# Cached keys and memory rows rearranged from DRAM to DRAM ahead of the attention of a decoder step, with new step numbers for the attention's loads

## The chip, the core and the metric

The kernel runs on one NeuronCore of a Trainium2 chip. The engines named below are TensorE (PE, matmuls; PEld is its weight load), VectorE (DVE), ScalarE (ACT), GpSimd (POOL) and SyncE (SP, which here only issues DMAs). Each engine works through its own instructions in their built order. The metric is the device time of one execution in microseconds (us), a median over executions of one kernel.

## What is computed

One layer of a decoder for 256 prompt tokens and 8 samples of 4 tokens, which share all weights (D_MODEL 2048, float32):

```python
z = rms_norm(x, g_mix) @ w_in                      # 2048 x 11264: branch inputs and gates
y_a, y_b, y_c = chunk_mixer(..), conv_module(..), pool_mixer(..)
x = x + sum(sigmoid(gate) * (y @ w_branch)) @ w_out
q = rms_norm(x, g_xattn) @ w_xq                    # 4 heads of 512
# prompt:  k, v = rms_norm(mem) @ w_xk, rms_norm(mem) @ w_xv     (256 memory rows)
# sample b: k, v = cache_mem_k[b], cache_mem_v[b]                (256 x 4 heads x 512 each)
x = x + (softmax(q k^T / sqrt(512)) v) @ w_xo
x = x + relu(rms_norm(x, g_mlp) @ w_up)^2 @ w_down
y = rms_norm(x, g_final)
```

The keys and values of the prompt are outputs too. The cached keys and values are 16 MB each, the memory `mem_prompt` is 2 MB, and all weights together are some 340 MB, each read once.

## The kernel before

**Weights.** A plan made ahead lists every weight in pieces of 512 rows x 512 columns (1 MB, a `raw` tile). `load_w` (line 154) has SP load a piece. `split_w` cuts a piece into two halves of 256 rows, and for each half ACT writes a rounded copy `w_hi` (line 172) and DVE the rest `w_lo` (line 173). TensorE then makes three matmuls for each 128 x 128 block of weights (hi x hi, hi x lo, lo x hi: lines 239 to 241 for the stages with all 288 tokens, lines 274 to 276 in `proj_mem` for the keys and values of the prompt, with the 256 memory rows as stationary side and 512 weight columns streaming). There are three `raw` buffers and three each of `w_hi` and `w_lo`. The split of a half needs the buffer of the half three before it, so it starts when TensorE has finished that one; the load of a piece needs a `raw` buffer whose two halves are both split.

**Steps.** A clock counts steps: one half of a weight is one step. `later(n, fn)` puts a piece of other work n steps ahead, `at(step, fn)` at a step counted from `base`, the step at which the projection with `w_xk` starts. The projections with `w_out` and `w_xq` are steps -64 to 0, `w_xk` is 0 to 32, `w_xv` 32 to 64, `w_xo` follows. All this only sets the order in which the instructions stand on each engine; what an engine does when is decided by its waits.

**Keys of the samples.** 32 blocks of 512 KB, one for each sample and head. `k_load(n)` fills one of six `kv` tiles (128 x 1024) by four DMAs (line 852), each of which reads pieces of 128 floats (512 B) from the cache into 32 partitions. `k_transposed(n)` (line 859) transposes the tile in 32 x 32 blocks on DVE into a `kT` tile (nine buffers), and `k_scores(b)` (line 874) runs 32 small matmuls for the four heads of sample b. Loads 0 to 14 are spread over steps -62 to -6; load n from 15 on stands right behind the transposition of block n - 6, whose tile it takes, and blocks 9 to 31 are transposed between steps 1.5 and 20. Values: `v_load` (line 995) fills the same six tiles, 4 KB a partition, and `sample_values(b)` (line 1003) runs 16 matmuls for each sample, at steps 24, 29, ..., 59.

**Memory rows.** In the last quarter of `w_xq`, `mem_load` (line 905) brings a quarter of the memory (256 rows x 512) into a `raw` buffer. `mem_transposed` has ACT square it with a sum along the row (line 913), TensorE transpose it in eight 128 x 128 blocks into PSUM (line 918), and ACT and DVE make `m1`, its rounded copy times a gain and the rest (lines 197 and 200).

Of the kernel before, what the change touches and what calls it, by code (L numbers as in the profile page):

```python
# [38 lines left out]
def decoder_step_kernel(  # L39
# [23 lines left out]
    k_scr = dram.tile([MEM, DM], F32, name="k_scr")  # L63

# [814 lines left out]
    def score_step(b):  # L879
        return 1 + 2.5 * b  # L880

    def value_step(b):
        return 24 + 5 * b

    def k_step(n):
        if n < 9:
            return 4 * n - 60
        return score_step((n - 9) // 4) + 0.5 + 0.3 * ((n - 9) % 4)

    for n in range(32):  # L890
        at(4 * n - 62 if n < 15 else k_step(n - 6) + 0.2, lambda n=n: k_load(n))
        at(k_step(n), lambda n=n: k_transposed(n))
# [8 lines left out]
    mss = small.tile([P, 2, 4], F32, name="mss")  # L901

    def mem_load(qr):
        mraw = wpool.tile([P, 4, 512], F32, name="mraw", tag="raw")
        nc.sync.dma_start(mraw[:, :2], mem_prompt[0, :, qr * 512:(qr + 1) * 512].rearrange("(c p) n -> p c n", p=P))
        mbox[qr] = mraw

    def mem_transposed(qr):
        m1.add()
        mraw = mbox[qr]  # L910
        for c in range(2):
            junk = small.tile([P, 512], F32, name="junk", tag="kn", bufs=3)
            s_.activation(junk, mraw[:, c, :], AF.Square, accum_out=mss[:, c, qr:qr + 1])
        for k2 in range(0, 4, 2):
            pt = psum()
            for d in range(2):
                for c in range(2):
                    t_.transpose(pt[:, d * 256 + c * P:d * 256 + (c + 1) * P],
                                 mraw[:, c, (k2 + d) * P:(k2 + d + 1) * P], ident)
# [4 lines left out]
    def mem_rstd():
        ms = small.tile([P, 3], F32, name="ms")
        v_.reduce_sum(ms[:, :2], mss, axis=AX.X)
        v_.tensor_scalar(ms[:, :2], ms[:, :2], 1.0 / DM, RMS_EPS, ALU.mult, ALU.add)
        rpow(r_mem, ms[:, :2])
# [144 lines left out]
    at(20, sample_softmax)  # L1073
    at(21, sample_probs)
# [171 lines left out]
```

## Time and profile before

| What | Value |
|---|---|
| median of 3 executions | 2170.93 us (2165.51 to 2171.38) |
| the profiled execution | 2167.95 us, its span 2166.1 us |
| PE busy, PEld busy | 2132.5 us (98%), 2060.2 us (95%) |
| DVE, ACT busy | 1284.6 us (59%), 865.1 us (40%) |
| bytes moved by DMA | 397.50 MB, mean 184 GB/s |
| largest groups of DMA issues | 87 of `w_in`, 64 of `w_up`, 64 of `w_down`, 1024 KB each; 128 of cached keys, 128 KB each; 32 of cached values, 512 KB each |

The span runs from the first to the last instruction. The page cuts it into 40 slices and gives the busy share of each engine in tenths; PE and PEld rows show whether TensorE has work at every moment, and the rows on the clock and on DMA show what it got. Waits are listed with the instruction that waited and what released it.

### The profile page before, as it was taken

The page shows a single profiled execution, that of the slowest core. Times are in us where ns is not written, and L with a number is a line of the kernel's source. Part 1 is how long each engine was busy: PE and PEld are TensorE (multiplying, and loading weights), DVE is VectorE, ACT ScalarE, POOL GpSimd, SP SyncE. Part 2 cuts the span into 40 slices and gives each one's busy share as a digit, 9 for nine tenths or more (in the row PEclk, how much of TensorE's full clock was granted, in tenths as well). Part 3 has the DMA queues.
Part 4 walks back from the last instruction along what each step waited for, and adds up shares of the span by engine and source line. Part 5 has one row for each costly group of instructions (what it writes and reads, how often), then busy time and mean ns, then how long its engine had stood idle before and what let it go on. Part 6 is the DMA issues. An engine that isn't in the chain of part 4 may idle for free.

```text
span 2166.1 us, 36855 instructions
## 1 busy us (share of the span) xinstructions
PE 2132.5 (98%) x15559; PEld 2060.2 (95%) x15559; DVE 1284.6 (59%) x1955; ACT 865.1 (40%) x1189; POOL 31.3 (1%) x93
## 2 busy tenths in 40 slices
PE   8999999999999999998899999999999999999998
PEld 7999999999999999995677899999999999999997
DVE  7767877677565657555555646554454445545554
ACT  5444433343345434352334534333333333333343
POOL 1000000000000000001000000000000000000000
PEclk9999999999999999999899999999999999999999
DMA  7546444544545577769998554545554555455542
GB/s 248 192 150 212 159 156 156 168 164 158 174 157 174 201 216 206 203 195 233 284 335 278 178 167 157 174 158 174 157 174 157 174 158 173 159 172 160 172 156 103
DMA packets 223417, 397.50 MB, mean 184 GB/s; under 512 B 9402, under 2 KB 47930, under 8 KB 222843
## 3 DMA queue, kind: packets, MB, share of 16 engines
q1 hardware_dynamic: 218117, 384.37, 55.8%
q10 hardware_dynamic: 4878, 10.72, 1.4%
q8 instruction: 122, 2.00, 0.4%
q14 instruction: 44, 0.36, 0.1%
q0 software_dynamic: 256, 0.05, 0.0%
HBM read 383.51 MB, written 12.80 MB: 183 GB/s over the span
## 4 chain that ended last, share of the span: by engine, by line
PE 56%; issue 38%; DMA 4%; DVE 1%; SPq 1%; ACT 0%; POOL 0%; ACTq 0%; POOLq 0%; DVEq 0%
PE ps L241 15%; PE ps L239 15%; PE ps L240 15%; PE ps L274 2%; PE ps L275 2%; PE ps L276 2%; DMA kv<-in_cache_mem_k_dram 1%; DMA raw<-in_w_xk_dram 1%; PE ps L1003 1%; SPq L852 0%; DMA raw<-in_w_in_dram 0%; DVE w_lo L173 0%; PE ps L647 0%; ACT w_hi L172 0%; DMA k_scr<-kn 0%
## 5 line engine op out<-in xcount | busy, mean ns | idle before, releaser
L173 DVE TENSOR_TENSOR w_lo<-raw,w_hi 128x1024 fp32r<-128x1024 f32 (+1 forms) x673 | 785.5, 1172 | 818.3 <-ACT w_hi L172 815.4
L172 ACT CAST w_hi<-raw 128x1024 fp32r<-128x1024 f32 (+1 forms) x673 | 673.4, 1007 | 1156.6 <-PE ps L240 964.0
L239 PE MATMUL ps<-q_hi,w_hi 128*128 128x288 f32 x3200 | 946.9, 296 | 1.7 <-ACT w_hi L172 1.2
L241 PE MATMUL ps<-q_hi,w_lo 128*128 128x288 f32 x3200 | 943.7, 295 | 1.2 <-DVE w_lo L173 1.2
L240 PE MATMUL ps<-q_lo,w_hi 128*128 128x288 f32 x3200 | 943.4, 295 | 0.7 <-DVE q_lo L200 0.7
L239 PEld LDWEIGHTS ps<-q_hi,w_hi 128*128 128x128 f32 x3200 | 601.0, 188 | 3.1 <-ACT w_hi L172 1.4
L240 PEld LDWEIGHTS ps<-q_lo,w_hi 128*128 128x128 f32 x3200 | 601.2, 188 | 1.5 <-DVE q_lo L200 0.9
L241 PEld LDWEIGHTS ps<-q_hi,w_lo 128*128 128x128 f32 x3200 | 600.6, 188 | 1.7 <-DVE w_lo L173 1.6
L241 PE MATMUL ps<-h_hi,w_lo 128*128 128x288 f32 x1024 | 302.2, 295 | 0.0
L239 PE MATMUL ps<-h_hi,w_hi 128*128 128x288 f32 x1024 | 301.9, 295 | 0.0
L240 PE MATMUL ps<-h_lo,w_hi 128*128 128x288 f32 x1024 | 301.5, 294 | 0.0
L239 PEld LDWEIGHTS ps<-h_hi,w_hi 128*128 128x128 f32 x1024 | 192.1, 188 | 0.0
L240 PEld LDWEIGHTS ps<-h_lo,w_hi 128*128 128x128 f32 x1024 | 192.1, 188 | 0.0
L241 PEld LDWEIGHTS ps<-h_hi,w_lo 128*128 128x128 f32 x1024 | 192.1, 188 | 0.0
L274 PE MATMUL ps<-w_hi,q_hi 128*128 128x512 f32 x256 | 102.7, 406 | 11.4 <-ACT w_hi L172 11.4
L241 PE MATMUL ps<-y_hi,w_lo 128*128 128x288 f32 x384 | 113.3, 295 | 0.0
L240 PE MATMUL ps<-y_lo,w_hi 128*128 128x288 f32 x384 | 113.1, 294 | 0.0
L239 PE MATMUL ps<-y_hi,w_hi 128*128 128x288 f32 x384 | 113.0, 294 | 0.0
L527 DVE SCALAR_TENSOR_TENSOR cv<-glu,cwT,cv 128x256 f32<-128x256 f32 x240 | 105.9, 478 | 0.0
L275 PE MATMUL ps<-w_lo,q_hi 128*128 128x512 f32 x256 | 103.0, 402 | 1.7 <-DVE w_lo L173 1.7
L276 PE MATMUL ps<-w_hi,q_lo 128*128 128x512 f32 x256 | 101.5, 397 | 0.0
L274 PEld LDWEIGHTS ps<-w_hi,q_hi 128*128 128x128 f32 x256 | 48.6, 192 | 29.3 <-ACT w_hi L172 16.9
(301 smaller groups left out, 1277.1 us busy)
## 6 DMA issues: line engine op xcount, KB each, us to landing
raw<-in_w_in_dram SPq DMA_DIRECT2D x87, 1024.0 KB
raw<-in_w_up_dram SPq DMA_DIRECT2D x64, 1024.0 KB
raw<-in_w_down_dram SPq DMA_DIRECT2D x64, 1024.0 KB
raw<-in_w_branch_dram SPq DMA_DIRECT2D x24, 1024.0 KB
raw<-in_w_out_dram SPq DMA_DIRECT2D x16, 1024.0 KB
kv<-in_cache_mem_k_dram SPq DMA_DIRECT2D x128, 128.0 KB
raw<-in_w_xq_dram SPq DMA_DIRECT2D x16, 1024.0 KB
raw<-in_w_xk_dram SPq DMA_DIRECT2D x16, 1024.0 KB
```

Source lines behind the costliest of these rows:

```text
L172: latest["hi"] = s_.copy(dh, src)
L173: latest["lo"] = v_.tensor_tensor(dl, src, dh.bitcast(F32), ALU.subtract)
L239: t_.matmul(o, wh, act.hi(kt), start=kt == 0, stop=False)
L240: t_.matmul(o, wh, act.lo(kt), start=False, stop=False)
L241: t_.matmul(o, wl, act.hi(kt), start=False, stop=kt == nkt - 1)
L274: t_.matmul(acc[c], mh, hi[:, i, :], start=kt == 0, stop=False)
L275: t_.matmul(acc[c], mh, lo[:, i, :], start=False, stop=False)
L276: t_.matmul(acc[c], ml, hi[:, i, :], start=False, stop=kt == KT - 1)
L527: v_.scalar_tensor_tensor(o, i, wk, o, ALU.mult, ALU.add)
L1003: t_.matmul(sbox["osc"][32 * h:32 * h + 32, :], pTm[:, c, h, :], vraw[4 * b + 2 * c + h // 2][:, (h % 2) * 512:(h % 2 + 1) * 512], start=b ...
```

## The change

Three things are done.

1. **Copies.** `key_blocks` and `mem_blocks` are new. During the branches SP issues 128 DMAs of 128 KB (one each 1.4 steps from step 12 of the kernel on) that copy the cached keys from DRAM to DRAM, in pieces of 512 B, into 32 blocks `k_blk` in the layout of a `kv` tile; and 64 DMAs of 32 KB (one each 2.8 steps) that do so with the memory, in pieces of 128 B, into four blocks `m_blk`.
2. **Loads and the transposition of the memory.** `k_load` is then one DMA of 128 rows of 4 KB. `mem_load` reads a quarter of the memory in one DMA of 128 rows of 4 KB into one half of the `raw` tile, DVE transposes it in 32 x 32 blocks into the other half, and `m1` is made from there; the 32 transpositions by TensorE are gone. The sums of squares are made from four loads of 512 KB of `mem_prompt` at steps -63 to -61.5.
3. **Step numbers.** The scores of samples 4 to 7 move from steps 11 to 18.5 to steps 12, 18.5, 25 and 31.5; the values from 24 + 5b to 34.5 + 3.6b; key loads 15 to 31 stand at 1, 2.65, ..., 27.4, one each 1.65 steps; value loads 0.8 steps apart; the memory loads each one step earlier.

```diff
+    k_blk = [dram.tile([P, 1024], F32, name=f"k_blk{n}") for n in range(32)]
+    m_blk = [dram.tile([P, 1024], F32, name=f"m_blk{n}") for n in range(4)]
...
+    def mem_blocks(qr, k, qd):
+        c0 = qr * 512 + k * P + qd * 32
+        nc.sync.dma_start(m_blk[qr][32 * qd:32 * qd + 32, k * 256:(k + 1) * 256].rearrange("p (m r) -> p m r", r=32),
+                          mem_prompt[0, :, c0:c0 + 32].rearrange("(m p) r -> p m r", p=32))
+
+    def key_blocks(n, qd):
+        b, h = divmod(n, 4)
+        nc.sync.dma_start(k_blk[n][32 * qd:32 * qd + 32].rearrange("p (m r) -> p m r", r=P),
+                          cache_mem_k[0, b, :, h, qd * P:(qd + 1) * P].rearrange("(m p) r -> p m r", p=32))
+    for n in range(32):
+        for qd in range(4):
+            later(12 + (4 * n + qd) * 1.4, lambda n=n, qd=qd: key_blocks(n, qd))
+    for n in range(64):
+        later(12.5 + n * 2.8, lambda n=n: mem_blocks(n // 16, n // 4 % 4, n % 4))
...
+    mss = small.tile([P, 2, 2], F32, name="mss")
+
+    def mem_squares(c, half):
+        kv = kv_tile()
+        nc.sync.dma_start(kv, mem_prompt[0, c * P:(c + 1) * P, half * 1024:(half + 1) * 1024])
+        later(2, lambda: s_.activation(kv, kv, AF.Square, accum_out=mss[:, c, half:half + 1]))
...
     def k_load(n):
-        b, h = divmod(n, 4)
         kv = kv_tile()
-        for qd in range(4):
-            nc.sync.dma_start(
-                kv[32 * qd:32 * qd + 32].rearrange("p (m r) -> p m r", r=P),
-                cache_mem_k[0, b, :, h, qd * P:(qd + 1) * P].rearrange("(m p) r -> p m r", p=32))
+        nc.sync.dma_start(kv, k_blk[n])
         kraw[n] = kv
...
     def score_step(b):
-        return 1 + 2.5 * b
+        return 1 + 2.5 * b if b < 4 else 12 + 6.5 * (b - 4)
 
     def value_step(b):
-        return 24 + 5 * b
+        return 34.5 + 3.6 * b
+
+    def k_load_step(n):
+        return 3.9 * n - 59 if n < 15 else 1 + 1.65 * (n - 15)
 
     def k_step(n):
         if n < 9:
-            return 4 * n - 60
-        return score_step((n - 9) // 4) + 0.5 + 0.3 * ((n - 9) % 4)
+            return 3.9 * n - 56
+        return max(score_step((n - 9) // 4) + 0.5 + 0.3 * ((n - 9) % 4), k_load_step(n) + 2)
 
     for n in range(32):
-        at(4 * n - 62 if n < 15 else k_step(n - 6) + 0.2, lambda n=n: k_load(n))
+        at(k_load_step(n), lambda n=n: k_load(n))
         at(k_step(n), lambda n=n: k_transposed(n))
...
     def mem_load(qr):
         mraw = wpool.tile([P, 4, 512], F32, name="mraw", tag="raw")
-        nc.sync.dma_start(mraw[:, :2], mem_prompt[0, :, qr * 512:(qr + 1) * 512].rearrange("(c p) n -> p c n", p=P))
+        nc.sync.dma_start(mraw[:, :2], m_blk[qr].rearrange("p (t n) -> p t n", t=2))
         mbox[qr] = mraw
 
     def mem_transposed(qr):
         m1.add()
-        mraw = mbox[qr]
-        for c in range(2):
-            junk = small.tile([P, 512], F32, name="junk", tag="kn", bufs=3)
-            s_.activation(junk, mraw[:, c, :], AF.Square, accum_out=mss[:, c, qr:qr + 1])
-        for k2 in range(0, 4, 2):
-            pt = psum()
-            for d in range(2):
-                for c in range(2):
-                    t_.transpose(pt[:, d * 256 + c * P:d * 256 + (c + 1) * P],
-                                 mraw[:, c, (k2 + d) * P:(k2 + d + 1) * P], ident)
-            for d in range(2):
-                kt = 4 * qr + k2 + d
-                split_act_gain(m1.hi(kt), m1.lo(kt), pt[:, d * 256:(d + 1) * 256], gmem[:, kt:kt + 1])
+        mraw = mbox.pop(qr).rearrange("p t n -> p (t n)")
+        mT = mraw[:, 1024:]
+        v_.transpose(mT, mraw[:, :1024])
+        for k in range(4):
+            kt = 4 * qr + k
+            split_act_gain(m1.hi(kt), m1.lo(kt), mT[:, k * 256:(k + 1) * 256], gmem[:, kt:kt + 1])
...
-                later(2 * qr + 1, lambda qr=qr: mem_load(qr))
+                later(2 * qr, lambda qr=qr: mem_load(qr))
...
-        at(k_step(26 + n) + 0.2 if n < 6 else value_step((n - 6) // 4) + 0.5 + (n - 6) % 4, lambda n=n: v_load(n))
+        at(28.5 + 0.8 * n if n < 6 else value_step((n - 6) // 4) + 0.3 + 0.8 * ((n - 6) % 4), lambda n=n: v_load(n))
```

How the instructions stand, at three places. Names carry the number of their tile (`raw_10394` is one weight piece, `kv_10656` one key block); a row with x4 is four equal DMAs.

**SP during the first pieces of `w_xk`.** Before:

```order
L154 DMA raw_10737<-in_w_xk_dram 128x4x512
L852 DMA kv_10656<-in_cache_mem_k_dram 32x8x128 x4
L852 DMA kv_10663<-in_cache_mem_k_dram 32x8x128 x4
L852 DMA kv_10682<-in_cache_mem_k_dram 32x8x128 x4
L852 DMA kv_10695<-in_cache_mem_k_dram 32x8x128 x4
L852 DMA kv_10749<-in_cache_mem_k_dram 32x8x128 x4
L852 DMA kv_10756<-in_cache_mem_k_dram 32x8x128 x4
L852 DMA kv_10769<-in_cache_mem_k_dram 32x8x128 x4
L852 DMA kv_10786<-in_cache_mem_k_dram 32x8x128 x4
L154 DMA raw_10816<-in_w_xk_dram 128x4x512
L852 DMA kv_10873<-in_cache_mem_k_dram 32x8x128 x4
L154 DMA raw_10887<-in_w_xk_dram 128x4x512
```

With the change:

```order
L156 DMA raw_10803<-in_w_xk_dram 128x4x512
L886 DMA kv_10765<-k_blk15_86 128x1024
L886 DMA kv_10825<-k_blk16_87 128x1024
L156 DMA raw_10864<-in_w_xk_dram 128x4x512
L886 DMA kv_10878<-k_blk17_88 128x1024
L886 DMA kv_10909<-k_blk18_89 128x1024
L156 DMA raw_10927<-in_w_xk_dram 128x4x512
L886 DMA kv_10963<-k_blk19_90 128x1024
L156 DMA raw_10976<-in_w_xk_dram 128x4x512
```

Before, eight key blocks (32 DMAs) stand between two weight pieces of `w_xk`, then four; with the change it is at most two (two DMAs).

**SP from the end of `w_xq` to the start of `w_xk`.** Before:

```order
L154 DMA raw_10306<-in_w_xq_dram 128x4x512
L905 DMA mraw_10338<-in_mem_prompt_dram 128x2x512
L154 DMA raw_10394<-in_w_xk_dram 128x4x512
L905 DMA mraw_10426<-in_mem_prompt_dram 128x2x512
L154 DMA raw_10482<-in_w_xk_dram 128x4x512
L905 DMA mraw_10512<-in_mem_prompt_dram 128x2x512
L154 DMA raw_10601<-in_w_xk_dram 128x4x512
L154 DMA raw_10668<-in_w_xk_dram 128x4x512
L154 DMA raw_10737<-in_w_xk_dram 128x4x512
```

With the change:

```order
L938 DMA mraw_10471<-m_blk0_103 128x1024
L938 DMA mraw_10503<-m_blk1_104 128x1024
L156 DMA raw_10505<-in_w_xq_dram 128x4x512
L886 DMA kv_10578<-k_blk14_85 128x1024
L938 DMA mraw_10580<-m_blk2_105 128x1024
L156 DMA raw_10582<-in_w_xk_dram 128x4x512
L938 DMA mraw_10655<-m_blk3_106 128x1024
L156 DMA raw_10657<-in_w_xk_dram 128x4x512
L156 DMA raw_10744<-in_w_xk_dram 128x4x512
L156 DMA raw_10803<-in_w_xk_dram 128x4x512
```

Weight and memory loads alternate in both; the first two memory loads now stand ahead of the last `w_xq` piece. All of them take one of the three `raw` buffers, and which one is fixed when the program is built. Before, the first two `w_xk` pieces (`raw_10394`, `raw_10482`) take the buffers of the last two `w_xq` pieces (`raw_10237`, `raw_10306`), each of which has its second split three halves ahead of the first split of the piece that takes it. With the change `raw_10505` (the last of `w_xq`), `raw_10582` and `raw_10657` (the first two of `w_xk`) go one after the other through one buffer, ahead of them the memory tile `mraw_10471`: each waits for the second split of the piece before it, one half ahead of its own first split.

**DVE at the same place.** Before:

```order
L173 TENSOR_TENSOR w_lo_10397<-raw_10306,w_hi_10396 128x4x4x32 x2
L173 TENSOR_TENSOR w_lo_10453<-raw_10306,w_hi_10452 128x4x4x32 x2
L200 SCALAR_TENSOR_TENSOR q_lo1_10429<-ps_10434,gmem_87,q_hi1_10428 128x256
L200 SCALAR_TENSOR_TENSOR q_lo1_10429<-ps_10443,gmem_87,q_hi1_10428 128x256
L200 SCALAR_TENSOR_TENSOR q_lo1_10429<-ps_10434,gmem_87,q_hi1_10428 128x256
L200 SCALAR_TENSOR_TENSOR q_lo1_10429<-ps_10443,gmem_87,q_hi1_10428 128x256
L173 TENSOR_TENSOR w_lo_10485<-raw_10394,w_hi_10484 128x1024
L173 TENSOR_TENSOR w_lo_10539<-raw_10394,w_hi_10538 128x1024
```

With the change:

```order
L175 TENSOR_TENSOR w_lo_10585<-raw_10505,w_hi_10584 128x4x4x32 x2
L945 STREAM_TRANSPOSE mraw_10503<-mraw_10503 128x1024
L175 TENSOR_TENSOR w_lo_10626<-raw_10505,w_hi_10625 128x4x4x32 x2
L202 SCALAR_TENSOR_TENSOR q_lo1_10615<-mraw_10503,gmem_123,q_hi1_10614 128x256 x4
L175 TENSOR_TENSOR w_lo_10660<-raw_10582,w_hi_10659 128x1024
L945 STREAM_TRANSPOSE mraw_10580<-mraw_10580 128x1024
L175 TENSOR_TENSOR w_lo_10699<-raw_10582,w_hi_10698 128x1024
L202 SCALAR_TENSOR_TENSOR q_lo2_10688<-mraw_10580,gmem_123,q_hi2_10687 128x256 x4
L945 STREAM_TRANSPOSE mraw_10655<-mraw_10655 128x1024
L202 SCALAR_TENSOR_TENSOR q_lo3_10731<-mraw_10655,gmem_123,q_hi3_10730 128x256 x4
L175 TENSOR_TENSOR w_lo_10747<-raw_10657,w_hi_10746 128x1024
L175 TENSOR_TENSOR w_lo_10784<-raw_10657,w_hi_10783 128x1024
```

The transpositions of the memory tiles (`mraw<-mraw`) now stand between the splits of the weight halves; before, only the gain steps (`q_lo` from `ps`) did.

More of the change, by code (lines that the diff above doesn't have):

```diff
@@ L843, in kv_tile, with mem_rstd @@
         return kv
+    mss = small.tile([P, 2, 2], F32, name="mss")
[3 more added lines that the diff above has]
+        later(2, lambda: s_.activation(kv, kv, AF.Square, accum_out=mss[:, c, half:half + 1]))
+    def mem_rstd():
+        ms = small.tile([P, 3], F32, name="ms")
+        v_.reduce_sum(ms[:, :2], mss, axis=AX.X)
+        v_.tensor_scalar(ms[:, :2], ms[:, :2], 1.0 / DM, RMS_EPS, ALU.mult, ALU.add)
+        rpow(r_mem, ms[:, :2])
+    for c in range(2):
+        for half in range(2):
+            at(c + 0.5 * half - 63, lambda c=c, half=half: mem_squares(c, half))
+    at(-58, mem_rstd)
     kraw, kts = {}, {}
     def k_load(n):
-        b, h = divmod(n, 4)
         kv = kv_tile()
-        for qd in range(4):
-            nc.sync.dma_start(
-                kv[32 * qd:32 * qd + 32].rearrange("p (m r) -> p m r", r=P),
-                cache_mem_k[0, b, :, h, qd * P:(qd + 1) * P].rearrange("(m p) r -> p m r", p=32))
+        nc.sync.dma_start(kv, k_blk[n])
         kraw[n] = kv
@@ L900, in decoder_step_kernel @@
     mbox = {}
-    mss = small.tile([P, 2, 4], F32, name="mss")
     def mem_load(qr):
         mraw = wpool.tile([P, 4, 512], F32, name="mraw", tag="raw")
-        nc.sync.dma_start(mraw[:, :2], mem_prompt[0, :, qr * 512:(qr + 1) * 512].rearrange("(c p) n -> p c n", p=P))
+        nc.sync.dma_start(mraw[:, :2], m_blk[qr].rearrange("p (t n) -> p t n", t=2))
         mbox[qr] = mraw
@@ L909, in mem_transposed @@
         m1.add()
-        mraw = mbox[qr]
-        for c in range(2):
-            junk = small.tile([P, 512], F32, name="junk", tag="kn", bufs=3)
-            s_.activation(junk, mraw[:, c, :], AF.Square, accum_out=mss[:, c, qr:qr + 1])
-        for k2 in range(0, 4, 2):
-            pt = psum()
-            for d in range(2):
-                for c in range(2):
-                    t_.transpose(pt[:, d * 256 + c * P:d * 256 + (c + 1) * P],
-                                 mraw[:, c, (k2 + d) * P:(k2 + d + 1) * P], ident)
-            for d in range(2):
-                kt = 4 * qr + k2 + d
-                split_act_gain(m1.hi(kt), m1.lo(kt), pt[:, d * 256:(d + 1) * 256], gmem[:, kt:kt + 1])
[L924 to L928, printed above, removed]
+        mraw = mbox.pop(qr).rearrange("p t n -> p (t n)")
[4 more added lines that the diff above has]
+            split_act_gain(m1.hi(kt), m1.lo(kt), mT[:, k * 256:(k + 1) * 256], gmem[:, kt:kt + 1])
     def gmem_load():
@@ L952, in decoder_step_kernel @@
     mem_transposed(3)
-    mem_rstd()
     assert clock[0] == base
@@ L1071, in head_values @@
         s_.copy(q[:, 4 * h + d, :NP], po[:, :NP])
-    at(20, sample_softmax)
-    at(21, sample_probs)
+    at(32.5, sample_softmax)
+    at(33.5, sample_probs)
     for b in range(NB):
@@ L1078, in decoder_step_kernel @@
     for n in range(32):
-        at(k_step(26 + n) + 0.2 if n < 6 else value_step((n - 6) // 4) + 0.5 + (n - 6) % 4, lambda n=n: v_load(n))
-    at(60, sample_out)
-    at(60.5, sample_out2)
+        at(28.5 + 0.8 * n if n < 6 else value_step((n - 6) // 4) + 0.3 + 0.8 * ((n - 6) % 4), lambda n=n: v_load(n))
+    at(61, sample_out)
+    at(61.5, sample_out2)
     act = Quarters()
```

## The prediction

> **What bounds the kernel now.** I read the page's tenths first, for the one place where TensorE is not full.
>
> ```profile
> PE 2132.5 (98%) x15559; PEld 2060.2 (95%) x15559; DVE 1284.6 (59%) x1955; ACT 865.1 (40%) x1189; POOL 31.3 (1%) x93
> PE   8999999999999999998899999999999999999998
> PEld 7999999999999999995677899999999999999997
> PEclk9999999999999999999899999999999999999999
> DMA  7546444544545577769998554545554555455542
> ```
>
> A slice is 54.2 us. TensorE sets the pace everywhere but in slices 19 to 23, where PE and the clock dip while the DMA engines are full. Then the table of busy time by stretch, which has the instructions, the granted clock, the DMA share and GB/s in its last columns:
>
> ```profile
> 560.00:640.00 80.00, 80.00 (x604) 79.70 (x603) 45.81 (x71) 31.82 (x41) 1.86 (x2) 1.00 0.50 166
> 974.00:1000.00 26.00, 26.00 (x185) 18.89 (x184) 18.59 (x21) 8.67 (x13) 3.60 (x9) 1.00 1.05 233
> 1000.00:1072.00 72.00, 58.46 (x333) 39.70 (x332) 37.82 (x38) 16.68 (x18) 2.67 (x6) 0.91 1.01 282
> 1072.00:1105.00 33.00, 33.00 (x161) 24.46 (x160) 14.59 (x14) 10.89 (x11) 1.40 (x6) 1.00 0.85 302
> 1105.00:1228.00 123.00, 123.00 (x669) 96.26 (x668) 75.25 (x115) 59.03 (x96) 2.77 (x8) 1.00 0.78 257
> ```
>
> 974 to 1105 is the projection `w_xk`, 1105 to 1228 `w_xv`. Only 1000 to 1072 has an idle PE (13.5 us) and a clock below 1.00. The waits of 960 to 1260 (total us, times, longest) name what came late:
>
> ```profile
> ACT w_hi L172 <- DMA raw<-in_w_xk_dram: 51.0, 6, 14.3
> PE ps L274 <- ACT w_hi L172: 11.4, 3, 7.3
> ```
>
> ACT waits for weights of `w_xk`, PE for ACT: eight key blocks of 512-byte pieces stand in SP's order between two weight pieces, and the queue was full of them:
>
> ```profile
> DMA packets 6245, 3.25 MB, mean 217 GB/s; under 512 B 366, under 2 KB 6102, under 8 KB 6243
> q1 hardware_dynamic: 6243, 3.23, 119.6%
> ```
>
> (983 to 998: 15 us x 16 engines x 1.196 / 6243 packets = 46 ns of an engine per piece.)
>
> How much is lost there? The matmuls of the stretch 973.85 to 1105.0 by line, and four rows of the timeline at its ends and at the score and value blocks:
>
> ```profile
> L275 PE MATMUL ps<-w_lo,q_hi 128*128 128x512 f32 x128 | 52.9, 413 | 1.7 <-DVE w_lo L173 1.7
> L874 PE MATMUL ps<-kT,qm 128*32 128x256 f32 x256 | 17.7, 382 | 0.4 <-DVE kT L859 0.4
> 973.90 0.48 PE L274 MATMUL ps<-w_hi,q_hi 128*128 128x512 f32 x1
> 976.84 1.93 PE L874 MATMUL ps<-kT,qm 128*32 128x256 f32 x32
> 978.71 0.50 PE L274 MATMUL ps<-w_hi,q_hi 128*128 128x512 f32 x1
> 1104.12 0.39 PE L276 MATMUL ps<-w_hi,q_lo 128*128 128x512 f32 x1
> 1105.03 0.39 PE L274 MATMUL ps<-w_hi,q_hi 128*128 128x512 f32 x1
> ```
>
> From 1104.12 to 1105.03 four matmuls start, 0.2275 us each. 3 x 128 of them are 87.4 us. A score block costs 1.96 (978.71 less 976.75, when the next matmul would have started); eight are 15.7, and the two value blocks at about the same price 3.9. That is 106.9 of the 131.1 us from 973.90 to 1105.03: **24.2 us are stall and half clock**. `w_xv`, 123 us at a full PE, has none.
>
> **The change, part by part.**
>
> *Key loads as 4 KB rows, spread out: −24.2.* With the change at most two block loads stand between two weight pieces. In `w_xk` a step is 106.9 / 32 = 3.3 us and asks for 0.5 MB of weights and 0.32 MB of keys (one block per 1.65 steps), plus 1 MB of prompt keys written per 8 steps: 0.99 MB per 3.3 us, some 300 GB/s. The 1072 row moved 302 GB/s at a share of 0.85 with PE full. So it fits, but not by much; the same holds in `w_xv`, where value loads come 0.9 steps apart (about 0.5 + 0.58 MB per 3.7 us with its value block, 290 GB/s). For the unevenness I add **+1.5** (0 to 6).
>
> *Memory transposed by DVE: −4.5.* The 32 transposes by PE go. One of four groups:
>
> ```profile
> 973.05 0.86 PEld L918 LDWEIGHTS ps<-ident,mraw 128*128 128x128 f32 x8 [1.25 <-issue]
> 973.08 1.06 PE L918 MATMUL ps<-ident,mraw 128*128 128x128 f32 x8 [1.05 <-DMA mraw<-in_mem_prompt_dram]
> ```
>
> 4 x 0.86 is 3.4, and the wait of 1.05 that the last group had goes too. ACT's eight squares move to the projection with `w_out`, where ACT is 40% busy; nothing waits there.
>
> *The new order of the `raw` buffers: +5.0.* As the orders above show, the last `w_xq` piece (I call it Q3) and the first two of `w_xk` (X0, X1) go through one buffer. Each is issued only when the second split of the one before is made, one half before its own first. The rows for this chain:
>
> ```profile
> 950.22 1.14 ACT L172 CAST w_hi<-raw 128x512 fp32r<-128x512 f32 x2 [2.04 <-PE ps L240]
> 950.87 1.29 DVE L173 TENSOR_TENSOR w_lo<-raw,w_hi 128x512 fp32r<-128x512 f32 x2 [1.88 <-ACT w_hi L172]
> 954.44 0.83 ACT L197 ACTIVATE q_hi<-ps,gmem 128x256 fp32r<-128x256 f32 x2
> 955.26 0.87 DVE L200 SCALAR_TENSOR_TENSOR q_lo<-ps,gmem,q_hi 128x256 fp32r<-128x256 f32 x2
> 964.74 1.05 ACT L172 CAST w_hi<-raw 128x1024 fp32r<-128x1024 f32 x1 [0.85 <-PE ps L240]
> 965.83 1.23 DVE L173 TENSOR_TENSOR w_lo<-raw,w_hi 128x1024 fp32r<-128x1024 f32 x1 [1.42 <-ACT w_hi L172]
> 979.17 1.24 DVE L859 STREAM_TRANSPOSE kT<-kv 128x1024 f32<-128x1024 f32 x1
> ```
>
> A half lasts 3.18 us (950.22 to 953.40, the next cast). The issue of a weight to its landing takes 4.75 us: one issued at 563.45 moved its bytes from 564.2 to 568.2.
>
> ```profile
> 563.45 6.73 SPq L154 DMA_DIRECT2D raw<-in_w_in_dram  x2
> 563.40:564.20 0.80, 0.80 (x8) 0.80 (x7) 0.02 (x1) 0.00 (x0) 0.00 (x0) 1.00 0.00 0
> 564.20:568.20 4.00, 4.00 (x32) 4.00 (x31) 1.23 (x1) 1.78 (x2) 0.00 (x0) 1.00 0.81 262
> 568.20:569.60 1.40, 1.40 (x13) 1.40 (x12) 1.04 (x1) 0.32 (x1) 0.00 (x0) 1.00 0.05 12
> ```
>
> On the clock of the old trace: after the split at 950.87 to 952.16 DVE transposes the first memory tile (1.24, the price of a key block of the same 128 x 1024) and ACT and DVE make its gains (about 0.42 and 0.44 each, four of each) until about 955.7; Q3 is issued, lands at 960.5, and PE does not wait. Its second split ends about 965.0, with a transposition (1.24) ahead of it on DVE. X0 lands at 969.7; cast 1.05 and split 1.23 bring 972.1, PE multiplies a half about two halves after its cast: the half cast at 950.22 from 956.5 on, Q3 is the third and fourth half from there, and PE has used it up at 956.5 + 4 x 3.18 = 969.2: **2.7 us** idle, with a little of the cast's overlap off. X0's second split stands behind the next transposition and ends at 974.6, X1 lands at 979.4, is split at 981.8, and PE is ready at about 979.4: **2.3 us**. From X2 on the pieces take other buffers. The bounds: 0, if the second splits run ahead of the transpositions' waits, to 9, if the gains of a tile (1.7 us) also push each second split back.
>
> *The clock after these waits: +2.4.* In the 1000 row 13.5 us of idle time went with a clock of 0.91, that is 0.09 x 72 = 6.5 us of speed lost, about 0.48 per idle us; 0.48 x 5.0 = 2.4. Bounds 0 (the 1.05 us wait at 973.08 is followed by 1.00 in the 974 row) to 6.5. The Trainium skill, "TensorE: Matmul & The Clock Gate", section "What's actually happening", has the half clock begin after an idle window of about 3.4 us; by that rule neither wait here brings it, and the sum would be 2.4 lower. In the old trace the idle times and the dip of the clock stand in one stretch, which doesn't separate long waits from short.
>
> *The copies in the branches: 0, beside PE.* 128 DMAs x 256 pieces of 512 bytes and 64 DMAs x 256 pieces of 128 bytes, from step 12 to 191, while the queue has a share of 0.50 (the 560 row). No row of the old trace shows this copy. Lower bound per piece: DRAM-to-DRAM copies of the states at 162 to 176, where
>
> ```profile
> q10 hardware_dynamic: 38, 1.21, 21.9%
> ```
>
> is 1.21 MB in 14 x 16 x 0.219 = 49 engine-us, 24.6 GB/s per engine, or 21 ns per 512 bytes. Upper: the 46 ns of the key pieces above, which also had a small piece on the SBUF side. In 6.36 us (one weight piece) stand 1.43 key and 0.71 memory DMAs, 34 pieces per engine: 0.7 to 1.6 us beside 0.50 x 6.36 = 3.2. Weights have time to spare:
>
> ```profile
> 561.11 1.05 ACT L172 CAST w_hi<-raw 128x1024 fp32r<-128x1024 f32 x1 [1.79 <-PE ps L240]
> 577.01 1.05 ACT L172 CAST w_hi<-raw 128x1024 fp32r<-128x1024 f32 x1 [2.13 <-PE ps L240]
> ```
>
> With three buffers, the piece issued at 563.45, after the half cast at 561.11, is wanted by the cast five halves later, at 577.01; it landed at 568.2, 8.8 us early. So I take 0. The cover is gone when a piece takes (6.36 − 3.2) x 1000 / 34 = 93 ns; above that each further 10 ns costs 34 x 0.01 us per period, times 89 periods, 30 us. Against the gain of some 21 us the change breaks even at 100 ns.
>
> The Trainium skill, "DMA: Bandwidth & Descriptors", section "Specifications", wants at least 512 bytes for line rate and says that below it the engine reads, modifies and writes. It speaks against the memory's 128-byte pieces; were these to cost twice 46 ns, a period would have 11.4 x 46 ns = 0.5 us more, still covered. The sum would be the same; the slower rival gains some of its chance from it.
>
> **The sum** on the profiled execution (2167.95, 1.9 around its span): 2167.95 − 24.2 − 4.5 + 1.5 + 5.0 + 2.4 = 2148.2. The median of the runs shown is 3.0 above that execution and the lowest run 2.4 below it, so runs of the changed kernel may lie as far to either side. I say **2148**, its own range 2142 to 2154.
>
> **The rivals.**
>
> *No wait at the handover* (DVE and ACT get there earlier than I drew it): 2148.2 − 7.4 = **2141**. For it: PE's idle is the difference of two long chains, each good to a microsecond or two. Against: the lead of one half is built in.
>
> *The transfers still bind in `w_xk`*: keys, weights and the written prompt keys ask for some 300 GB/s, and the 1000 row is full at 282. If half of the 24.2 stays: 2148.2 − 1.5 + 12.1 = **2159**. Against: the 1072 row moves 302 with room.
>
> *The change doesn't do what it says*: the stall stays because the key loads wait for their `kv` tile (six, as before) and the weights behind them in SP's order wait along. Only the transposes go, and the handover takes that back: 2168 − 4.5 + 7.4 = **2171** (2163 without the handover). Against: a load each 1.65 steps frees a tile in time, two steps before the transposition.
>
> *Slower: the copies starve the weights.* A weight piece queues behind the copies on SP's one queue. It decides above 100 ns per piece; at 150 ns, 34 x 0.150 = 5.1 us beside 3.2 is 1.9 us too much per 6.36, times 89 periods, 172 us: 2148 + 172 = **2320**. For it: pieces with a small end on both sides stand nowhere in the trace, and a third of the pieces are of 128 bytes only. Against: 46 ns is a price with one small side and one queue full, and twice that is still covered.
>
> **How the numbers follow.** Forecast 0.46, no handover wait 0.21, transfers bind 0.17, not what it says 0.08, slower 0.08. The range takes in the first three with their bounds, 2138 to 2164, and leaves out little more than 0.16. A measurement of this kernel tells 0.3% (6.5 us) from no change: faster than 2164.4 are the first three cases but for a little of the third, 0.83; within, 0.09; slower, 0.08.
>
> **What would show it.** In the tenths, PE 9 in slices 19 to 22. In `w_xk`, some 112 us from its first to its last matmul in place of 131.1, and no long waits of ACT for `in_w_xk` but two short ones in its first 10 us. In the branches a DMA share of 0.60 to 0.75 with PE full; any wait of PE there says that the price of a piece is wrong. The forecast fails if `w_xk` stays above 120 us, or if PE idles at the start of `w_xk` not at all or by over 9 us.

## The result

The changed kernel took 2146.76 us in the median of four executions against 2171.15 us before (four executions), 24.4 us less. One of the four took 6568.9 us; it did not come back in the four later executions of the same kernel (2143.46 to 2145.29, median 2144.84), and its cause is not known. Without it the median is 2145.47 us; the ratio to the kernel before, taken without it, is 0.9889 with a 95% interval of 0.9871 to 0.9908. The profiled execution took 2144.98 us, its span is 2143.2.

The page of the changed kernel, the same rows as before:

```profile
PE 2122.3 (99%) x15527; PEld 2054.1 (96%) x15527; DVE 1288.3 (60%) x1959; ACT 864.7 (40%) x1181; POOL 31.3 (1%) x93
PE   8999999999999999999999999999999999999998
PEld 7999999999999999996777999999999999999997
PEclk9999999999999999999999999999999999999999
DMA  7757565666665566658989545555554555555542
```

The dip of PE in slices 19 to 23 is gone. In the table by stretch (granted clock, DMA share and GB/s are the last three columns) the branches, the handover from `w_xq` to `w_xk`, and `w_xk` itself read:

```profile
560.00:640.00 80.00, 80.00 (x604) 79.70 (x604) 45.98 (x70) 31.82 (x41) 1.87 (x2) 1.00 0.62 197
956.00:985.00 29.00, 26.90 (x195) 21.12 (x194) 19.27 (x30) 12.36 (x21) 1.93 (x6) 0.94 0.67 229
985.00:1068.00 83.00, 83.00 (x480) 64.42 (x479) 60.08 (x54) 27.83 (x27) 3.93 (x8) 1.00 0.96 330
```

PE is full beside a share of 0.62 in the branches, and full in `w_xk` from 985 on. Of these three only the handover, 956 to 985, has an idle PE and a lower clock. The waits of 940 to 1240:

```profile
ACT w_hi L174 <- DMA raw<-in_w_xk_dram: 6.6, 3, 4.7
ACT w_hi L174 <- DMA raw<-in_w_xq_dram: 4.7, 1, 4.7
PE ps L276 <- ACT w_hi L174: 2.1, 1, 2.1
```

ACT waited 51.0 us for weights of `w_xk` before and waits 6.6 now.

```profile
971.05 1.20 PE L276 MATMUL ps<-w_hi,q_hi 128*128 128x512 f32 x2 [2.10 <-ACT w_hi L174]
1077.62 0.39 PE L276 MATMUL ps<-w_hi,q_hi 128*128 128x512 f32 x1
```

These are the first matmul of `w_xk` and the first of `w_xv` (1077.62): 106.6 us between them, 131.1 before. `w_xv` takes 127.5 (before 123.0), and two more of the eight value blocks (3.7 us) now stand in it. From the first matmul of `w_xo` to the last of the program it is 927.53 us in both.

### The profile page after: what moved, and what is told of

Its sections match the earlier page's. It is cut to its first block, busy times and chain, and to the rows that moved or that the text cites. A ratio compares the mean times of both kernels' runs of the same rounds, so it can differ in the third digit from the quotient of the medians.

```text
span 2143.2 us, 36818 instructions
## 1 busy us (share of the span) xinstructions
PE 2122.3 (99%) x15527; PEld 2054.1 (96%) x15527; DVE 1288.3 (60%) x1959; ACT 864.7 (40%) x1181; POOL 31.3 (1%) x93
## 4 chain that ended last, share of the span: by engine, by line
PE 59%; issue 38%; DVE 1%; DMA 1%; ACT 0%; SPq 0%; POOL 0%; POOLq 0%; ACTq 0%; DVEq 0%
PE ps L243 15%; PE ps L241 15%; PE ps L242 15%; PE ps L276 3%; PE ps L277 3%; PE ps L278 3%; PE ps L906 1%; PE ps L1022 1%; DMA raw<-in_w_in_dram 0%; DVE w_lo L175 0%; PE ps L665 0%; DMA raw<-in_w_xk_dram 0%; DMA raw<-in_w_xq_dram 0%; ACT w_hi L174 0%; PE ps L1089 0%
## 5 line engine op out<-in xcount | busy, mean ns | idle before, releaser
L241 PEld LDWEIGHTS ps<-y_hi,w_hi 128*128 128x128 f32 x384 | 72.1, 188 | 0.0
```

What stands on the lines that cost most here:

```text
L241: t_.matmul(o, wh, act.hi(kt), start=kt == 0, stop=False)
```

## Experiments

The table takes from the trace of each run the time from the first matmul of `w_xk` to the first of `w_xv`, that of `w_xv`, into how many pieces the eight score and eight value blocks are cut on TensorE (the same in the built order), and the median time of one packet of a key load between 984 and 1068 us. In the kernel before, in the two runs made from it by adding copies, and with the old steps, `w_xk` holds two value blocks (3.7 us) that stand in `w_xv` in the others. All columns but the median come from one profiled execution, which lies up to 7.3 us from the median of its kernel (2166.01 against 2173.30 in the last row). The kernel before, run again beside the others, took 2169.11 to 2169.48 us in the median; the ratios below are to these.

| kernel | median us | w_xk | w_xv | score, value pieces | key packet |
|---|---|---|---|---|---|
| before | 2171.15 | 131.1 | 123.0 | 10, 8 | 512 B, 44 ns |
| changed, first and second profile | 2146.76, 2144.84 | 106.6, 105.0 | 127.5 | 9, 8 | 4 KB, 159 ns |
| steps alone | 2172.46 | 123.5 | 137.4 | 17, 20 | 512 B, 46 ns |
| rows, old steps | 2149.86 | 115.3 | 123.0 | 15, 8 | 4 KB, 159 ns |
| memory loads three steps apart | 2141.66 | 104.5 | 127.5 | 8, 8 | 4 KB, 159 ns |
| copies alone | 2168.53 | 134.6 | 123.0 | 10, 8 | 512 B, 46 ns |
| copies in 128-byte pieces | 2210.84 | 130.1 | 123.0 | 10, 8 | 512 B, 44 ns |
| old memory path | 2147.24 | 103.9 | 127.5 | 8, 8 | 4 KB, 159 ns |
| quarter loads, 32 partitions in a row | 2168.03 | 117.3 | 137.3 | 19, 20 | 4 KB, 262 ns |
| quarter loads, every fourth partition | 2164.25 | 116.4 | 137.4 | 19, 20 | 4 KB, 159 ns |
| quarter loads, 128 partitions | 2146.10 | 106.6 | 127.5 | 9, 8 | 1 KB, 46 ns |
| half loads in 512-byte pieces, 128 partitions | 2145.05 | 106.5 | 127.5 | 9, 8 | 512 B, 27 ns |
| steps alone, TensorE held in order | 2173.30 | 115.9 | 137.0 | 8, 8 | 512 B, 45 ns |

The theory at the start was that of the prediction: 512-byte pieces are dear (46 ns of a DMA engine each), and eight blocks of them in SP's order hold up the weights.

**The steps alone.** The kernel before with the new step numbers:

```diff
     def score_step(b):
-        return 1 + 2.5 * b
+        return 1 + 2.5 * b if b < 4 else 12 + 6.5 * (b - 4)
...
-        at(4 * n - 62 if n < 15 else k_step(n - 6) + 0.2, lambda n=n: k_load(n))
+        at(k_load_step(n), lambda n=n: k_load(n))
...
```

> The kernel before with the new step numbers alone: the key blocks still come in 512-byte pieces, one block each 1.65 steps, and the memory goes through TensorE. Theory A (the stall is the time the pieces take on the DMA engines, spread or not): 17 blocks x 1024 pieces x 46 ns / 16 engines are 49 us, 16 weight pieces of w_xk at 4.0 us x 0.81 are 52 us, and the prompt's keys come on top, so w_xk asks for about its whole 107 us; some of the stall stays, w_xk takes 112 to 125 us, 2150 to 2163 in all. Rival B (only the bursts in SP's order hurt, the piece size does not matter): w_xk 107 to 109 us, 2144 to 2149. Rival C (the steps do nothing): w_xk 131, 2165 to 2171.

2172.46 us (ten executions), ratio 1.0012 (0.9999 to 1.0025): even spreading gains nothing by itself, about as rival C had the time. But `w_xk` is shorter (123.5, within theory A's range) and `w_xv` is longer (137.4), of which none of the theories spoke. The queue is as full as before, and ACT still waits for weights:

```profile
974.00:1000.00 26.00, 25.35 (x187) 18.38 (x186) 20.81 (x26) 10.19 (x15) 4.25 (x9) 1.00 1.02 250
1040.00:1080.00 40.00, 35.01 (x176) 24.64 (x175) 18.62 (x18) 9.72 (x10) 0.77 (x2) 0.96 1.05 235
ACT w_hi L172 <- DMA raw<-in_w_xk_dram: 43.7, 7, 11.4
```

**The rows with the old steps.** The changed kernel with the step numbers of the kernel before, but for those of the memory loads.

```diff
-        at(k_load_step(n), lambda n=n: k_load(n))
+        at(4 * n - 62 if n < 15 else k_step(n - 6) + 0.2, lambda n=n: k_load(n))
...
```

> The changed kernel with the old step numbers: copies and 4 KB rows, but eight and then four key blocks stand between two weight pieces again, and values go at the old steps. Theory A: a burst of eight blocks is 4.2 MB, at 330 GB/s 12.7 us, while a weight piece has about 9 us to spare; a stall of some 4 us at the first burst and little at the second, w_xk about 110 to 114 us with the two value blocks in it, 2146 to 2152. Rival B (bursts are all): most of the 24 us comes back, 2160 to 2168. Rival C (pieces are all, bursts cost nothing): 2143 to 2146, as the changed kernel.

2149.86 us, ratio 0.9906 (0.9888 to 0.9924): within theory A's time. Of the 24.4 us between the kernel before (2169.26 beside it) and the changed kernel (2144.84), the copies, the loads in rows and the memory's new path carry some 19 without the steps, and the steps some 5 on top of them. That the 5 us are bursts on the queue, as A had it, is not shown: behind its first matmul PE idles in `w_xk` for hardly a microsecond

```profile
1000.00:1072.00 72.00, 71.99 (x422) 50.05 (x421) 45.58 (x45) 22.54 (x24) 4.10 (x12) 1.00 0.94 337
```

while the built order cuts the score blocks into 15 pieces, and these take 19.2 us in place of 15.9 in the second profile of the changed kernel.

**The handover.** The memory loads about three steps apart and each transposition two steps behind:

```diff
-                later(2 * qr, lambda qr=qr: mem_load(qr))
-            for qr in range(3):
-                later(2 * qr + 3, lambda qr=qr: mem_transposed(qr))
+                later((2, 5, 8, 10.5)[qr], lambda qr=qr: mem_load(qr))
+                later((4, 7, 10, 12.5)[qr], lambda qr=qr: mem_transposed(qr))
...
-    mem_transposed(3)
```

> The changed kernel with the memory loads at steps 2, 5, 8, 10.5 of the last quarter of w_xq (its 8 steps; the last two stand in w_xk) and their transpositions two steps behind each, in place of 0, 2, 4, 6 and 3, 5, 7, 8. In the built order each weight piece then waits for a split three halves ahead, or for gains that are as far ahead, and none for one a single half ahead. Theory A (the wait of 2.3 us at the start of w_xk and the half clock behind it come from the lead of one half in the raw buffers): both go, 2.3 + 1.8 = 4 us, 2141 against 2145 for the changed kernel. Rival: the wait comes from DVE and ACT doing the memory's transpositions and gains at that place, whatever the buffers; it stays or moves into w_xk, 2145 to 2149.

> The changed kernel as it is, beside the others on the same chip. 2145 to 2148; w_xk 106.6 us from its first matmul to that of w_xv, one wait of 2.3 us ahead of it.

2141.66 us (2140.15 to 2143.25) against 2144.84 (2143.46 to 2145.29) for the changed kernel beside it: 3.2 us less, the fastest kernel here, 0.987 (0.9853 to 0.9886) of the time before. PE has no wait left at the handover, and 0.6 us in the 26 us behind it:

```profile
960.00:974.00 14.00, 14.00 (x100) 13.62 (x99) 10.53 (x20) 7.68 (x13) 0.00 (x0) 1.00 0.62 215
974.00:1000.00 26.00, 25.39 (x181) 18.35 (x180) 24.33 (x27) 10.56 (x15) 4.07 (x8) 1.00 0.80 273
957.88 0.37 SPq L156 DMA_DIRECT2D raw<-in_w_xk_dram  x1
```

(two rows of the table by stretch and one of SP's timeline). The first `w_xk` piece is issued at 957.88; in the changed kernel it was issued at 964.72, behind the split before it:

```profile
964.72 0.38 SPq L156 DMA_DIRECT2D raw<-in_w_xk_dram  x1
974.54 5.75 SPq L156 DMA_DIRECT2D raw<-in_w_xk_dram  x3
```

DVE and ACT do the same transpositions and gains in both, so their work alone does not make the wait; the order of the buffers does, as theory A said. The transpositions moved as well, though, and that share is not separated: in the changed kernel one of 1.24 us stands on DVE just ahead of the split that frees the buffer for the first `w_xk` piece.

```profile
962.28 1.24 DVE L945 STREAM_TRANSPOSE mraw<-mraw 128x1024 f32<-128x1024 f32 x1
963.44 1.25 DVE L175 TENSOR_TENSOR w_lo<-raw,w_hi 128x512 fp32r<-128x512 f32 x2
```

**The copies alone.** The kernel before, with the copies of the change put in and read by nothing. The orders on PE, ACT and SP (but for the copies) are those of the kernel before; on DVE a few rows of the branches change places.

```diff
...
+    for n in range(32):
+        for qd in range(4):
+            later(12 + (4 * n + qd) * 1.4, lambda n=n, qd=qd: key_blocks(n, qd))
+    for n in range(64):
+        later(12.5 + n * 2.8, lambda n=n: mem_blocks(n // 16, n // 4 % 4, n % 4))
```

> The kernel before with the copies of the change put into it; nothing reads them, keys and memory are loaded as before. Theory A (a piece takes some 22 ns of an engine, as the share of DMA in the branches of the changed kernel says: 0.62 against 0.50 over 80 us for 7272 more packets; all of it beside PE): no change, 2164 to 2172, PE full in the branches at a share near 0.62. Rival (the copies delay weights here and there): a few us more, 2173 to 2185.

2168.53 us (ten executions), ratio 0.9992 (0.9980 to 1.0005): they cost nothing that can be measured.

```profile
560.00:640.00 80.00, 80.00 (x603) 79.70 (x603) 45.82 (x70) 31.82 (x41) 1.87 (x2) 1.00 0.62 198
```

**Copies in 128-byte pieces**, also for the keys:

```diff
-        nc.sync.dma_start(k_blk[n][32 * qd:32 * qd + 32].rearrange("p (m r) -> p m r", r=P),
-                          cache_mem_k[0, b, :, h, qd * P:(qd + 1) * P].rearrange("(m p) r -> p m r", p=32))
+        for s in range(4):
+            c0 = qd * P + 32 * s
+            nc.sync.dma_start(k_blk[n][32 * qd:32 * qd + 32, 256 * s:256 * s + 256].rearrange("p (m r) -> p m r", r=32),
+                              cache_mem_k[0, b, :, h, c0:c0 + 32].rearrange("(m p) r -> p m r", p=32))
```

> As the run with the copies alone, but the keys are copied in pieces of 128 bytes as well: 512 DMAs of 256 pieces, four times as many. 103 pieces per engine stand then in a period of 6.36 us, which has 3.2 us free. Theory A (22 ns whatever the size of the piece): 2.3 us, hidden, 2165 to 2175, share in the branches about 0.85. Theory B (a small piece costs what a key piece does on its way into SBUF, 46 ns): 4.7 us, 1.5 us too much for 89 periods, about 2300. Theory C (a piece under 512 bytes costs twice 46): 9.5 us, 6 us too much, about 2700.

2210.84 us, ratio 1.0185 (1.0160 to 1.0209): 41 us slower, between A and B, though for another reason than either. The packets are cheap (median 13 ns for 128 bytes, 27 ns for 512 bytes in the copies of the changed kernel), and the queue has room:

```profile
560.00:640.00 80.00, 77.78 (x570) 76.76 (x570) 42.25 (x57) 26.34 (x31) 0.00 (x0) 0.98 0.66 184
547.00 5.40 SPq L443 DMA_DIRECT2D k_blk<-in_cache_mem_k_dram  x8
552.50 0.55 SPq L156 DMA_DIRECT2D raw<-in_w_in_dram  x1
```

The share is 0.66, but SP needs 5.4 us to issue eight copies ahead of a weight piece. From the first matmul to the first of `w_xk` this run takes 1009.0 us, the kernel before 970.1, so nearly all of the loss lies ahead of `w_xk`. The built orders of PE, DVE and ACT in the branches differ too in this run, so how much of the 41 us is SP's issue time and how much the order stays open.

**The old memory path.** The changed kernel with the memory loads, TensorE transposes and squares of the kernel before, and no copies of the memory.

```diff
-        nc.sync.dma_start(mraw[:, :2], m_blk[qr].rearrange("p (t n) -> p t n", t=2))
+        nc.sync.dma_start(mraw[:, :2], mem_prompt[0, :, qr * 512:(qr + 1) * 512].rearrange("(c p) n -> p c n", p=P))
...
-        v_.transpose(mT, mraw[:, :1024])
...
+                    t_.transpose(pt[:, d * 256 + c * P:d * 256 + (c + 1) * P],
+                                 mraw[:, c, (k2 + d) * P:(k2 + d + 1) * P], ident)
...
```

> The changed kernel with the memory path of before (loads of 256 rows x 512 one step later, 32 transposes on TensorE, squares beside them) and without the copies of the memory. Theory A (the terms of the sum): 3.4 us of transposes and a wait of about 1 us come back, the wait of 2.3 us at the start of w_xk and its half clock (up to 1.8) go; 2145 to 2147, the memory part of the change is worth nothing by itself. Rival (DVE and ACT are relieved, the memory part gains its 4.5 in full): 2149 to 2151.

2147.24 us (2144.62 to 2148.38), 0.9894 (0.9873 to 0.9915). Against the changed kernel (2145.47 without its long execution, and 2144.84) the memory part is worth some 2 us, against the kernel with the loads three steps apart 5.6. By theory A's terms it should have been about 0 and about 4; both came out some 2 us higher, which is less than the spread of this run's executions.

**What makes a key load slow.** Four runs change only the form of the load from `k_blk`: quarters of 4 KB rows into 32 partitions in a row, the same into every fourth partition, quarters of 1 KB pieces into all 128 partitions, and halves of 512-byte pieces into all 128. The edits of the four stand one below the other here:

```diff
-        nc.sync.dma_start(kv, k_blk[n])
+        for qd in range(4):   # quarter loads
+            nc.sync.dma_start(kv[32 * qd:32 * qd + 32], k_blk[n][32 * qd:32 * qd + 32])
+        for qd in range(4):   # every fourth partition
+            nc.sync.dma_start(kv[qd::4], k_blk[n][qd::4])
+        for qd in range(4):   # 128 partitions x 1 KB
+            cs = slice(256 * qd, 256 * qd + 256)
+            nc.sync.dma_start(kv[:, cs], k_blk[n][:, cs])
+        for a in range(2):    # 128 partitions, pieces of 512 bytes
+            dst, src = (t.rearrange("p (b a r) -> p a b r", a=2, r=P)[:, a] for t in (kv, k_blk[n]))
+            nc.sync.dma_start(dst, src)
```

> The changed kernel with each key block loaded by four DMAs of 32 partitions, as before, but in rows of 4 KB. Theory A (the small pieces made the old loads slow): no change, 2143 to 2147. Rival (a DMA into 32 partitions is slow whatever its pieces, 200 to 230 GB/s): w_xk 120 to 130 us, 2158 to 2170.

> The changed kernel with each key block loaded by four DMAs of 32 rows of 4 KB, but each into every fourth partition (qd, qd + 4, ...) in place of 32 partitions in a row; size, count and rows are those of the run with quarter loads (2168 us, w_xk 117 us, the loads at some 220 GB/s of a full queue, against 380 in the changed kernel). Theory D (32 partitions in a row are a narrow door, the same few of them for all 16 DMA engines): the loads go at 350 to 390 GB/s, w_xk 104 to 108, 2143 to 2148. Rival E (128 KB or 32 rows per DMA are too little to fill 16 engines): as the quarter loads, w_xk 112 to 120, 2160 to 2170.

> The changed kernel with each key block loaded by four DMAs of 128 KB again, each into all 128 partitions, in pieces of 1 KB. Theory D (partitions decide): w_xk 104 to 108, 2143 to 2148. Rival E (128 KB per DMA is too little, or four times as many DMAs on the queue): w_xk 112 to 120, 2160 to 2170. Rival A (small pieces): between the two, w_xk 108 to 112, about 2150.

> The changed kernel with each key block loaded by two DMAs into all 128 partitions in pieces of 512 bytes, the piece size of the kernel before. Theory D (partitions decide, not the pieces): 21 to 26 ns of an engine per piece, w_xk 104 to 109, 2143 to 2150. Rival A (pieces of 512 bytes into SBUF cost 46 ns wherever they go, as my prediction had it): w_xk 117 to 124, as in the run with the steps alone, 2165 to 2172.

Loads into all partitions keep the whole gain, with pieces of 1 KB (2146.10, ratio 0.9889, 0.9872 to 0.9905) and of 512 bytes (2145.05, 0.9887, 0.9873 to 0.9902). Their built orders on PE, DVE and ACT are those of the changed kernel, row for row, so this is a clean pair: **small pieces were not the cause**. Theory D holds for these two, and A and E fall. The 512-byte pieces of the kernel before also came from another place, the cache in place of `k_blk`; but the copies read these same pieces of the cache at 27 ns each. Quarters into 32 partitions lose it, in a row (2168.03, ratio 0.9997, 0.9985 to 1.0009) and spread (2164.25, 0.9978, 0.9969 to 0.9988); the times are those of the rivals of these runs (with every fourth partition theory D had 2143 to 2148), the reason is only in part. One row each of the table by stretch, 1000 to 1040, for quarters in a row, every fourth partition, 1 KB pieces and 512-byte pieces:

```profile
1000.00:1040.00 40.00, 39.24 (x209) 27.97 (x208) 24.92 (x23) 11.57 (x11) 1.90 (x4) 1.00 0.88 262
```

```profile
1000.00:1040.00 40.00, 39.24 (x210) 27.96 (x209) 26.05 (x24) 11.01 (x11) 1.90 (x4) 1.00 0.80 278
```

```profile
1000.00:1040.00 40.00, 40.00 (x247) 30.51 (x246) 26.12 (x24) 12.90 (x13) 2.29 (x6) 1.00 0.98 337
```

```profile
1000.00:1040.00 40.00, 40.00 (x247) 30.52 (x246) 27.23 (x25) 12.64 (x12) 3.01 (x7) 1.00 1.05 337
```

The first two have the same built orders; between them only the partitions differ, and with them the packets (262 and 159 ns) and 3.8 us. But with every fourth partition the packets are as fast as in the changed kernel and the queue is not full (0.80), and 10 us are lost in `w_xk` and 10 in `w_xv` all the same. There the **built order** is another one: from the score blocks on, TensorE's work is cut up. The order is made when the program is built, and the form of a load moves it: four loads into all partitions leave it as it was, four into 32 partitions do not. By what rule the builder does so no run shows. Timelines of that run at its first value block, which is whole, and at pieces of the fourth:

```profile
1095.46 0.72 PE L276 MATMUL ps<-w_hi,q_hi 128*128 128x512 f32 x2
1096.44 1.92 PE L1023 MATMUL ps<-kv,pTm 128*32 128x512 f32 x16 [0.26 <-POOL pTm L1007]
1098.30 0.50 PE L277 MATMUL ps<-w_lo,q_hi 128*128 128x512 f32 x1
```

```profile
1137.42 1.06 PE L1023 MATMUL ps<-kv,pTm 128*32 128x512 f32 x8
1139.08 1.04 PE L1023 MATMUL ps<-kv,pTm 128*32 128x512 f32 x2
```

The first block stands between a weight half's first matmuls and its next. A piece of two value matmuls takes as long as one of eight, so cutting costs time though nothing waits: in the whole of `w_xv` PE is idle for 0.4 us, and the value blocks take 22.3 us in 20 pieces, against 14.8 in eight. In `w_xk` the score blocks take 20.9 us against 16.7 in the first profile of the changed kernel, and PE is idle for 2.0 us; the rest of the 10 us is in the weights' matmuls between the pieces.

**TensorE held in order.** Was the cut order also what spoilt the steps alone? Each TensorE instruction from the start of `w_xk` to the end of `w_xv` is tied behind the one before it in the code:

```diff
+    real, last = t_, [None]
+
+    class InOrder:
+        def __getattr__(self, name):
+            def issue(*args, **kw):
+                with ExitStack() as order:
+                    if last[0] is not None:
+                        order.enter_context(tc.issue_after(last[0].ins))
+                    last[0] = getattr(real, name)(*args, **kw)
+                return last[0]
+            return issue
+    t_ = InOrder()
...
+    t_ = real
```

> The run with the steps alone (512-byte loads into 32 partitions, no copies, memory through TensorE), with TensorE held to the order in which the code issues its instructions during w_xk and w_xv: eight score blocks and eight value blocks in one piece each, where the built order of that run had cut them into 17 and 20 pieces. Theory F (of the 27 us that separated that run from the changed kernel, about 20 were the cut blocks, 10 in w_xk and 10 in w_xv, and about 7 the time that the old loads take on the DMA engines): w_xk 110 to 114, w_xv 127 to 128, 2150 to 2156. Rival A (the old loads fill the queue however TensorE is ordered): w_xk 120 to 125, 2160 to 2168. Rival B (the order was all): w_xk 104 to 107, 2144 to 2148, and the copies are not needed for the gain.

2173.30 us (twelve executions), ratio 1.0016 (1.0006 to 1.0027): theories F and B both fall, and it is a little slower still than rival A's range. The blocks are whole (8 and 8), the value blocks back at 14.8 us, and `w_xk` fell from 123.5 to 115.9; the rest of the time turned up as waits: ACT for `w_xk`, PE (all its rows bear the wrapper's line 966) for the splits behind it.

```profile
1040.00:1080.00 40.00, 33.86 (x164) 24.84 (x162) 20.25 (x18) 10.67 (x11) 0.00 (x0) 1.00 1.01 248
ACT w_hi L172 <- DMA raw<-in_w_xk_dram: 44.3, 9, 9.0
PE ps L966 <- DVE w_lo L173: 7.6, 7, 1.8
```

So with the old loads (45 ns per 512 bytes) the queue is full in `w_xk` and the weights come late in both orders of TensorE. The orders of DVE, ACT and SP were left to the builder here, and `w_xv` stays at 137.0, with 5.7 us of idle PE and a queue that is less than full; how much of that is the order of those engines was not separated.

## Why the prediction was right, and where it was not

The forecast was 2148, the measurement 2146.76; on the profiled execution 2148.2 was worked out and 2144.98 measured. Most of these 3.2 us are a second wait at the handover that did not come.

*Key loads, −24.2 with +1.5 left over.* The size was right: `w_xk` without value blocks is 103.1 us by the same terms (87.4 and 15.7), and it took 106.6 and 105.0, with the half clock of the handover in it; with the handover mended 104.5, so 1.4 are left over. `w_xk` and `w_xv` together fell by 20.1 us, with 1.7 of half clock against them; the two terms had 22.7. The "some 112 us" that were to show it in `w_xk` still had the two value blocks in them, 3.7 us, which the new steps move to `w_xv`. The cause was named wrongly. The step put the price on pieces of 512 bytes ("the 46 ns of the key pieces"); it belongs to loads into 32 partitions in a row: 512 bytes take 27 ns into 128 partitions and 44 to 46 into 32 in a row, and 4 KB take 159 and 262. That the number came out all the same is luck: the change does away with the small pieces and with the 32 partitions at once. The other half of the step, spreading, is worth nothing without the rows and about 5 us with them; without the rows it shortens `w_xk` by 4 us and loses 10 in `w_xv`, where TensorE's order is cut. And the step left out that the form of a load changes the built order of TensorE, which in the quarter loads costs most of the 20 us that are lost there.

*Memory by DVE, −4.5.* From the first matmul of the program to the first of `w_xk` the change saves 3.3 us (970.1 to 966.9), with the new wait in it (2.1 idle, 2.3 from when the next matmul was due): 5.5 without. Of these 0.9 come from the start, where the first 200 matmuls take 36.5 and 35.6 us, and anything from 35.0 to 38.8 in the runs here; 4.6 are left, and the term holds.

*The `raw` buffers, +5.0.* The first wait was foreseen at 2.7 and is 2.1 (2.2 in the second profile), X0's issue foreseen at the end of a split one half ahead, and so it was. The second, foreseen at 2.3, did not come, though its cause did: X1 was foreseen to be issued at 974.6 and was issued at 974.54. What failed is the sentence that "PE is ready at about 979.4". X0's 24 matmuls (0.2275 each) and one score block (1.96), begun behind the first wait at 969.2 + 2.7, end there; but two blocks stand ahead of X1 on TensorE, the second right in front of it, and PE did not want X1 before 983.4, when its split was made:

```profile
981.10 2.35 PE L906 MATMUL ps<-kT,qm 128*32 128x256 f32 x34
983.38 0.73 PE L276 MATMUL ps<-w_hi,q_hi 128*128 128x512 f32 x2
```

The half clock slowed the first of the two blocks. But in the second profile, at full clock, there is no second wait either.

*The clock, +2.4.* In the first profile the 3.6 us behind the wait run at 0.53, in the second at 1.00:

```profile
971.00:974.60 3.60, 3.55 (x14) 1.56 (x15) 3.57 (x4) 2.10 (x4) 0.00 (x0) 0.53 0.00 0
```

```profile
972.30:975.90 3.60, 3.60 (x21) 2.29 (x22) 3.60 (x4) 2.11 (x5) 0.00 (x0) 1.00 0.00 0
```

So the term is 1.7 or 0, and mis-sized mostly because there was one wait, not two. The rule of the Trainium skill that was weighed ("TensorE: Matmul & The Clock Gate", section "What's actually happening": an idle window of about 3.4 us brings the half clock) does not hold here as a bound: 2.10 us of idle PE brought it in one execution, and 2.23 us did not in the other. In five more runs PE is idle at this place, for 1.9 to 2.4 us, and the half clock comes behind it each time.

*The copies, 0.* Right: 27 ns per 512 bytes and 13 per 128, near the lower bound of 21 that was given, and no measurable cost; the doubled price that was weighed for 128 bytes did not come. The rival's point, 100 ns of an engine per piece, was the wrong one to watch: in the run with 512 copies of small pieces the kernel slows by 41 us at a DMA share of 0.66, with 13 ns per piece.

Of the rivals, "no wait at the handover" (2141) is the kernel with the memory loads three steps apart, 2141.66. "The transfers still bind" did not come: 330 GB/s at a share of 0.96 with PE full.

## What to carry to other kernels

Ask of a slow load into how many partitions one DMA writes, and whether they stand in a row, before blaming the size of its pieces, and read the time of a packet, not only the share. An edit to a DMA can make the builder rearrange TensorE's instructions; compare the built orders of two kernels before a difference is put down to the transfer. And when a tile takes a place in a buffer pool, follow who gets the next buffer and how far ahead: moving four loads and their transpositions by a few steps was worth 3 us here, without changing any work.

## What was not expected of the hardware

A packet of 4 KB takes 159 ns when four DMAs of 32 rows go to every fourth partition, and 262 ns when they go to 32 partitions in a row. Which part of the path is narrow there no run shows. A piece of two value matmuls, cut out of its block, takes as long as one of eight (1.04 and 1.06 us); why, no run shows. A load of the cached keys straight from the cache into all 128 partitions, without copies, was not tried.
